# A two-layer mixer and mixture-of-experts kernel: one-hot masks issued earlier, transposes one chunk later, and the first two mixer projections walked tile by tile

## The chip, the cores and the metric

The kernel runs on one NeuronCore of a Trainium2 chip. The metric is the device time of one execution in microseconds (us): 1666.42 us, the median of three runs (1659.75 to 1669.41). Five engines work side by side, each on its own list of instructions in order: PE (TensorE, matrix products), DVE (VectorE), ACT (ScalarE), POOL (GpSimd) and SP, which here only issues transfers (DMAs). They meet through semaphores: an instruction that waits holds up all that stands behind it on its engine.

## The reference

256 tokens of width 1024 pass through two layers. Each has a token mixer and then a feed-forward part, with a residual sum and a layer norm behind both. The first layer's feed-forward part is a dense SwiGLU, the second's a mixture of 8 experts of which each token takes 2.

```python
def token_mixer(x, ...):                     # w_in is 1024 x 9992
    h = x @ w_in + b_in
    a_q, a_k, a_v, b_u, b_v, c_qk, c_v, c_o, c_i, c_f, g_pre = split(h)
    ...                                      # attention y_a, spatial gating y_b
    qk = silu(causal_depthwise_conv(c_qk, conv_w, conv_b))
    ...                                      # chunkwise mLSTM on qk: y_c
    return (gates-weighted sum of y_a @ w_br_a, y_b @ w_br_b, y_c @ w_br_c) @ w_out

def moe_swiglu(x, router_w, router_b, w1, w3, w2):
    top_v, top_i = top_k(x @ router_w + router_b, 2)
    for e in range(8):
        out = out + gates[:, e:e+1] * ((silu(x @ w1[e]) * (x @ w3[e])) @ w2[e])
```

All data are float32. One expert has three weights of 1024 x 2816.

## The kernel before, in words

**Precision and chunks.** Every weight arrives by a DMA on SP's queue as a *chunk*, mostly 128 x 2048 numbers (1 MB), in the mixers' 384-column projections 128 x 1536. `weights` (line 115) then makes two parts of it: ACT casts the raw chunk to `wh` (L123) and DVE computes the rest `wl` = raw - wh (L125). Five raw chunks can be in place (`W_RAW`), four `wh` and four `wl`. Activations are split in the same way into `xh` and `xl`, and a product is xh*wh + xl*wh + xh*wl: three matmuls for each 128 rows of the weight (`mac`, L138 to L140, in the mixers and the dense part; L967 and L969 in the experts, where half of the work, that for the *light* experts, uses two of the three terms).

**PSUM.** Two rings of four banks: `mm` for products that accumulate, `tr` for transposes and other small results. A product's first matmul waits until whoever held its bank before has been read out.

**Experts.** `route` ranks the 8 experts by their number of tokens. The four largest are *heavy* (up to 128 slots), the others *light* (up to 64), and `moe` handles four pairs of one heavy and one light. Of each pair first the up products (three column groups, heavy and light in turn, once for w1 and once for w3), then 22 down chunks, heavy and light in turn. Tokens get into an expert's slots by a product with a one-hot mask: `onehots` (L805) makes the masks `op` of a pair with four DVE instructions (L811), and `gather` (L835) multiplies them with the tokens in eight pieces (L842) that ACT copies out (L844, L845). `moe` writes the order of PE, ACT and DVE by hand: `stream` (L928) goes from *job* to job, one weight chunk each. In a step it first issues the DMA, cast and subtraction of the chunk three steps ahead, then the products of its own chunk, then the *posts* due in this step, then one piece of side work (a gather piece, for example). A post is due so many steps behind the job it hangs on:

```python
for d, f in jobs[c].post:
    due.setdefault(c + d, []).append(f)
```

At the end of an up product the posts are: the eviction at once (`heavy`, L990 to L993; `light`, L1010 to L1013); for a light w1 product its SiLU one step later (L1034); after w3 the transposes and split of the result two steps later (`heavy_out`, L1001; `light_out`, L1022). `following`, which makes the next pair's masks and adds its gather to the side work, hangs on the first heavy down chunk, due at once.

## Time and profile before

| | |
|---|---|
| median of the runs | 1666.42 us (three runs, 1659.75 to 1669.41) |
| the profiled execution | 1661.5 us, its span 1659.8 us, mean granted TensorE clock 0.974 |
| busy share of the span | PE 94%, weight loads 81%, DVE 79%, ACT 61%, POOL 1% |
| transfers | 436.77 MB, 263 GB/s on average; 371 GB/s from 940 to 1640 us |
| stages | mixer of layer 0 to about 345 us, dense feed-forward to 545, mixer of layer 1 to 905, experts to 1640, last norm and output to the end |

A row of a timeline gives the start, the duration, engine, line, operation and tiles; the bracket at its end is how long the engine stood idle before, and what ended that. [...] A DMA share of 1 means that all 16 engines of the core had a packet under way.

### The profile page before, as it was taken

To read this page: it belongs to the slowest core of one execution; us is meant where nothing else is said; L and a number is where in the kernel's file an instruction comes from. 1 tells how busy PE (TensorE), PEld (TensorE's weight loads), DVE (VectorE), ACT (ScalarE), POOL (GpSimd) and SP (SyncE) were. 2 spreads that over 40 slices of the span, in tenths; PEclk is the share of its full clock that TensorE was granted. 3 is DMA by queue.
4 is the path that set the end of the run, shared out by engine and by line. 5 is a ranking of instruction groups with operands and counts; after the bars stand their busy time and mean duration, and the time that the engine had idled before them with its cause. 6 is when DMAs were issued, how large, how long until landed. Compare 5 with 4: busy or idle time off the path is not lost. (4 is left out here: it accounts for less than half of the span.)

```text
span 1659.8 us, 20819 instructions
## 1 busy us (share of the span) xinstructions
PE 1563.7 (94%) x7796; PEld 1336.8 (81%) x7796; DVE 1307.4 (79%) x1388; ACT 1015.5 (61%) x936; POOL 21.9 (1%) x98
## 2 busy tenths in 40 slices
PE   8899999999999999999999996999979997999995
PEld 7899978888887998987887876877867776877874
DVE  6868775774455866777578798899979998899997
ACT  4454673443343343576346786878878787878773
POOL 1000000000000000000000000000000000000000
PEclk9999999999999998999999998999989998999998
DMA  8555644754554564555563999999989999999994
GB/s 290 175 172 176 224 154 139 270 176 157 201 203 133 178 200 143 185 188 162 170 217 103 358 386 361 341 387 379 356 349 401 371 375 386 346 391 377 349 415 181
DMA packets 168804, 436.77 MB, mean 263 GB/s; under 512 B 9588, under 2 KB 56824, under 8 KB 168696
## 3 DMA queue, kind: packets, MB, share of 16 engines
q1 hardware_dynamic: 168696, 435.37, 72.6%
q8 instruction: 63, 1.03, 0.2%
q14 instruction: 45, 0.37, 0.1%
HBM read 434.29 MB, written 1.05 MB: 262 GB/s over the span
## 5 line engine op out<-in xcount | busy, mean ns | idle before, releaser
L125 DVE TENSOR_TENSOR wl<-raw,wh 128x2048 fp32r<-128x2048 f32 (+3 forms) x437 | 905.9, 2095 | 216.2 <-ACT wh L123 214.7
L123 ACT CAST wh<-raw 128x2048 fp32r<-128x2048 f32 (+3 forms) x437 | 761.2, 1755 | 375.0 <-PE mm L139 264.1
L138 PE MATMUL mm<-wh,xh 128*128 128x384 f32 (+3 forms) x1056 | 386.7, 367 | 2.9 <-ACT xh L149 2.9
L139 PE MATMUL mm<-wh,xl 128*128 128x384 f32 (+3 forms) x1056 | 386.2, 366 | 1.4 <-DVE xl L150 1.4
L140 PE MATMUL mm<-wl,xh 128*128 128x384 f32 (+3 forms) x1056 | 384.1, 364 | 0.0
L967 PE MATMUL mm<-wh,xh 128*128 128x512 f32 (+2 forms) x752 | 240.4, 382 | 6.6 <-DVE g L1059 3.7
L138 PEld LDWEIGHTS mm<-wh,xh 128*128 128x128 f32 x1056 | 200.5, 190 | 23.7 <-ACT xh L149 4.0
L139 PEld LDWEIGHTS mm<-wh,xl 128*128 128x128 f32 x1056 | 200.3, 190 | 21.6 <-DVE xl L150 2.0
L140 PEld LDWEIGHTS mm<-wl,xh 128*128 128x128 f32 x1056 | 200.3, 190 | 18.8 <-issue 0.3
L969 PE MATMUL mm<-wl,xh 128*128 128x512 f32 (+2 forms) x752 | 192.9, 379 | 1.6 <-DVE wl L125 1.5
L967 PEld LDWEIGHTS mm<-wh,xh 128*128 128x128 f32 x752 | 140.7, 190 | 32.1 <-DVE g L1059 6.0
L969 PEld LDWEIGHTS mm<-wl,xh 128*128 128x128 f32 x752 | 138.7, 189 | 27.8 <-DVE wl L125 4.8
L967 PE MATMUL mm<-wh,xl 128*128 128x512 f32 (+2 forms) x368 | 138.8, 379 | 0.0
L967 PE MATMUL mm<-wh,g 128*128 128x512 f32 x352 | 89.9, 396 | 0.0
L967 PEld LDWEIGHTS mm<-wh,xl 128*128 128x128 f32 x368 | 70.3, 191 | 11.2
L967 PEld LDWEIGHTS mm<-wh,g 128*128 128x128 f32 x352 | 65.7, 190 | 13.1
L967 PE MATMUL mm<-wh,gl 128*128 128x512 f32 x176 | 51.1, 408 | 0.0
L969 PE MATMUL mm<-wl,gl 128*128 128x512 f32 x176 | 50.4, 404 | 0.0
L842 PE MATMUL tr<-op,xt 128*128 128x256 f32 x128 | 24.0, 327 | 27.0 <-DVE op L811 27.0
L969 PE MATMUL mm<-wl,g 128*128 128x512 f32 x176 | 48.3, 393 | 0.2 <-DVE wl L125 0.2
L842 PEld LDWEIGHTS tr<-op,xt 128*128 128x128 f32 x128 | 21.7, 225 | 30.4 <-DVE op L811 28.7
L139 PE MATMUL mm<-wh,m 128*128 128x512 f32 x112 | 44.3, 395 | 0.0
(268 smaller groups left out, 1484.2 us busy)
## 6 DMA issues: line engine op xcount, KB each, us to landing
raw<-in_moe_w_dram SPq DMA_DIRECT2D x220, 1024.0 KB, 7.3
raw<-in_w_in_dram SPq DMA_DIRECT2D x68, 768.0 KB, 4.3
raw<-in_moe_w_dram SPq DMA_DIRECT2D x56, 768.0 KB, 6.5
raw<-in_ffn_w_dram SPq DMA_DIRECT2D x33, 1024.0 KB, 5.0
raw<-in_w_in_dram SPq DMA_DIRECT2D x24, 1024.0 KB, 5.1
raw<-in_w_out_dram SPq DMA_DIRECT2D x8, 1024.0 KB, 5.0
bias<-in_b_in_dram SPq DMA_DIRECT2D x34, 192.0 KB, 4.9
raw<-in_w_br_c_dram SPq DMA_DIRECT2D x8, 768.0 KB, 5.2
```

What stands on the lines that cost most here:

```text
L123: nc.scalar.copy(h, raw)
L125: nc.vector.tensor_tensor(lo, raw, h.bitcast(F32), OP.subtract)
L138: nc.tensor.matmul(ps, xh, wh, start=first, stop=False)
L139: nc.tensor.matmul(ps, xl, wh, start=False, stop=False)
L140: nc.tensor.matmul(ps, xh, wl, start=False, stop=last)
L842: nc.tensor.matmul(pt[:, b].rearrange("p e s -> p (e s)"), xt[t][i][:, c:c + P], po[:, t].rearrange("p e s -> p (e s)"), start=not t, stop ...
L967: nc.tensor.matmul(ps[u], t[:, k0 + j, :], h[:, j, c], start=first and j == i == 0, stop=False)
L969: nc.tensor.matmul(ps[u], W[0][:, k0 + j, :], lo[:, j, c], start=False, stop=last and j == kk - 1)
```

## The change

There are three edits. (1) In the experts, the next pair's masks are no longer made by `following` but by a post on the eighth job from the end of the pair's up products, in the last column group; `following` itself comes one step later (due 1 in place of 0); and the transposes and the light SiLU come one step later each (3 for 2, 2 for 1). (2) In both mixers the first two projections are done by a new function `proj2`: both weights are requested first, then tile 0 is multiplied with both, then tile 1 with both, and all four evictions are written behind. (3) In layer 0 `columns` is written before `consts`.

```diff
+    def proj2(self, w, bias, c0, n, X, evicts):
+        bs, ws, ps = [], [], []
+        for i in range(2):
+            b = self.p("bias", [P, n], F32, 2)
+            with self.tc.high_priority(LEAD):
+                self.nc.sync.dma_start(b, bcast(bias[c0 + i * n:c0 + (i + 1) * n]))
+            bs.append(b)
+            ws.append(self.wchunk(w, c0 + i * n, n))
+        for t in range(NT):
+            for i in range(2):
+                o = self.mm([P, n])
+                self.gemm(o, X[t], ws[i])
+                ps.append((i, t, o))
+        for i, t, o in ps:
+            evicts[i](t, o, bs[i])
...
-    def mixer(self, l, x, X):
+    def mixer(self, l, x, X, cols=None):
...
-        cols = self.columns(l)
+        cols = cols or self.columns(l)
...
-                self.proj(w, bias, C_QK + 768 * s + 384 * i, 384, X, ev)
-                self.pump()
+                evs.append(ev)
+            if s == 0:
+                self.proj2(w, bias, C_QK, 384, X, evs)
+            else:
+                for i in range(2):
+                    self.proj(w, bias, C_QK + 768 + 384 * i, 384, X, evs[i])
+                    self.pump()
...
+    def marks(self, p):
+        return self.onehots((p, HEAVY + p), self.rslot, (self.iota, self.iota2), F32R, "o", 1)
...
-                _, xh, xl, new = self.pair(xt, p + 1)
+                xh, xl, new = self.pair(xt, p + 1, marks.pop())
...
+            if not last:
+                jobs[-8].post.append((0, lambda p=p: marks.append(self.marks(p + 1))))
...
-            dh[0].post.append((0, lambda p=p: following(p)))
+            dh[0].post.append((1, lambda p=p: following(p)))
...
-            end.append((2, light_out if e.light else heavy_out))
+            end.append((3, light_out if e.light else heavy_out))
         elif e.light:
-            end.append((1, lambda: nc.scalar.activation(e.s, e.s, AF.Silu)))
+            end.append((2, lambda: nc.scalar.activation(e.s, e.s, AF.Silu)))
...
+            cols = net.columns(0)
             net.consts()
-            X = net.mixer(0, x, X)
+            X = net.mixer(0, x, X, cols)
```

What this moves, at three places. Line numbers in the changed kernel are 22 to 27 higher in the experts and 17 higher in `mixer` (its L864 is L842 before, L994 and L996 are L967 and L969, L1038 is L1011, L1049 is L1022, L833 is L811, L556 is L539).

The first place is PE at the end of the first pair's up products: `mm_8342` and `mm_8343` are the two banks of the last light up product (`mm_8346`, `mm_8347` in the changed kernel), `g` and `gl` are what the heavy and the light down product multiply, `tr ... op, xt` is the gather. Before:

```order
L969 MATMUL mm_8343<-wl_8340,xh_7471 128x384
L967 MATMUL mm_8411<-wh_8354,g_1332_7530 128x512
...
L969 MATMUL mm_8412<-wl_8356,g_1332_7530 128x512
L842 MATMUL tr_8435<-op_8425,xt_1241_7165 128x256
...
L967 MATMUL mm_8448<-wh_8373,gl_7934 128x512
...
L969 MATMUL mm_8449<-wl_8375,gl_7934 128x512
L1022 MATMUL tr_8458<-ident_70,hs_8298 128x128 x3
L842 MATMUL tr_8464<-op_8425,xt_1242_7166 128x256
```

and in the changed kernel:

```order
L996 MATMUL mm_8347<-wl_8344,xh_7471 128x384
L994 MATMUL mm_8416<-wh_8359,g_1332_7530 128x512
...
L996 MATMUL mm_8417<-wl_8361,g_1332_7530 128x512
L994 MATMUL mm_8436<-wh_8373,gl_7952 128x512
...
L996 MATMUL mm_8437<-wl_8375,gl_7952 128x512
L864 MATMUL tr_8451<-op_8270,xt_1241_7165 128x256
...
L994 MATMUL mm_8416<-wh_8392,g_1332_7530 128x512
...
L1049 MATMUL tr_8476<-ident_70,hs_8303 128x128 x3
```

The gather's first piece now stands behind the first light down product and no longer ahead of it, and the light transposes behind the second heavy one.

The second is DVE at the same place: the four mask instructions stand behind the light eviction (L1011) and one more subtraction before:

```order
L125 TENSOR_TENSOR wl_8389<-raw_8385,wh_8387 128x2048
L1011 TENSOR_TENSOR hs_8399<-mm_8342,hs_8399 64x384
L1011 TENSOR_TENSOR hs_8399<-mm_8343,hs_8399 64x384
L1013 TENSOR_TENSOR hs_8298<-hs_8298,hs_8399 128x384
L125 TENSOR_TENSOR wl_8409<-raw_8405,wh_8407 128x2048
L811 TENSOR_SCALAR op_8425<-iota_7171,so_7292 128x128
```

and in the changed kernel fifteen rows ahead of that eviction, in the middle of the last column group:

```order
L833 TENSOR_SCALAR op_8270<-iota_7171,so_7292 128x128
...
L125 TENSOR_TENSOR wl_8279<-raw_8275,wh_8277 128x1536
...
L125 TENSOR_TENSOR wl_8394<-raw_8390,wh_8392 128x2048
L1038 TENSOR_TENSOR hs_8404<-mm_8346,hs_8404 64x384
L1038 TENSOR_TENSOR hs_8404<-mm_8347,hs_8404 64x384
L1040 TENSOR_TENSOR hs_8303<-hs_8303,hs_8404 128x384
L125 TENSOR_TENSOR wl_8414<-raw_8410,wh_8412 128x2048
```

The light eviction itself keeps its place: it stands behind the subtraction `wl_8394` as it stood behind `wl_8389`.

The third is SP's queue at the start, where `raw` are weight chunks and the three rows from `conv_w` on are the convolution's columns. Before, they stood behind the fifteenth weight chunk:

```order
L121 DMA raw_777<-in_w_in_dram 128x4x384
L121 DMA raw_839<-in_w_in_dram 128x4x392
L239 DMA m_42_255<-in_conv_w_dram 48x128
L240 DMA m_42_255<-in_conv_b_dram 12x128
L241 DMA m_42_255<-in_sg_b_dram 6x128
```

and in the changed kernel behind the sixth:

```order
L295 DMA bias_265<-in_b_in_dram 128x384
L121 DMA raw_267<-in_w_in_dram 128x4x384
L295 DMA bias_279<-in_b_in_dram 128x384
L121 DMA raw_273<-in_w_in_dram 128x4x384
...
L121 DMA raw_432<-in_w_in_dram 128x4x384
L239 DMA m_13_104<-in_conv_w_dram 48x128
L240 DMA m_13_104<-in_conv_b_dram 12x128
L241 DMA m_13_104<-in_sg_b_dram 6x128
```

PE's transpose of the columns moves with them, from behind the first tile of the fourth projection (168 matmuls) to behind 52 matmuls, and one bias row now goes out ahead of the first weight chunk.

## Rows read from the trace of the kernel before

**Rows 1.** The page: busy time of each engine, its share, and its instructions.

```profile
PE 1563.7 (94%) x7796; PEld 1336.8 (81%) x7796; DVE 1307.4 (79%) x1388; ACT 1015.5 (61%) x936; POOL 21.9 (1%) x98
```

**Rows 2.** Stages: window, length, busy PE, PEld, DVE, ACT, POOL; clock, DMA, GB/s.

```profile
560.00:628.00 68.00, 68.00 (x394) 67.31 (x394) 51.73 (x77) 35.94 (x35) 0.00 (x0) 1.00 0.64 202
940.00:1018.00 78.00, 70.44 (x338) 58.22 (x337) 76.14 (x51) 62.52 (x50) 0.00 (x0) 0.98 0.98 362
1018.00:1208.00 190.00, 174.52 (x806) 144.95 (x805) 173.66 (x116) 147.58 (x123) 0.00 (x0) 0.96 0.98 371
```

**Rows 3.** What PE waited for: total us, times, longest.

```profile
PE tr L842 <- DVE op L811: 27.0, 4, 8.2
PE tr L1022 <- DVE hs L1013: 15.2, 9, 2.1
PE tr L1001 <- DVE hs L991: 8.4, 8, 1.7
```

**Rows 4.** Timeline of PE at the second pair boundary.

```profile
1211.55 1.07 PE L969 MATMUL mm<-wl,g 128*128 128x512 f32 x4
1220.35 1.40 PE L842 MATMUL tr<-op,xt 128*128 128x256 f32 x4 [7.72 <-DVE op L811]
...
1226.44 2.01 PE L967 MATMUL mm<-wh,g 128*128 128x512 f32 x8
...
1229.20 0.64 PE L842 MATMUL tr<-op,xt 128*128 128x256 f32 x4
1229.67 1.09 PE L967 MATMUL mm<-wh,gl 128*128 128x512 f32 x4
...
1231.51 0.64 PE L842 MATMUL tr<-op,xt 128*128 128x256 f32 x4
```

**Rows 5.** Timeline of DVE and ACT at the same boundary.

```profile
1215.97 1.13 DVE L1011 TENSOR_TENSOR hs<-mm,hs 64x384 f32<-64x384 f32 x2
...
1219.82 0.87 DVE L811 TENSOR_SCALAR op<-iota,so 128x128 fp32r<-128x128 f32 x4
1224.16 2.29 DVE L125 TENSOR_TENSOR wl<-raw,wh 128x2048 fp32r<-128x2048 f32 x1 [3.47 <-ACT wh L123]
...
1221.79 0.37 ACT L844 CAST xh<-tr 128x256 fp32r<-128x256 f32 x1 [5.41 <-PE tr L842]
```

**Rows 6.** Windows as in Rows 2: stretches of low clock, and transfers.

```profile
47.28:52.22 4.94, 4.94 (x22) 4.85 (x23) 4.05 (x11) 2.90 (x6) 0.00 (x0) 0.50 0.21 62
547.46:550.60 3.14, 3.14 (x10) 3.14 (x11) 1.83 (x3) 0.44 (x1) 0.00 (x0) 0.50 0.46 123
1171.80:1175.20 3.40, 3.40 (x10) 2.62 (x10) 3.40 (x3) 3.39 (x4) 0.00 (x0) 0.50 0.80 261
1208.00:1224.00 16.00, 8.28 (x33) 6.84 (x32) 12.30 (x14) 9.94 (x11) 0.00 (x0) 0.76 1.02 421
1224.00:1234.00 10.00, 10.00 (x47) 8.43 (x47) 6.89 (x4) 7.08 (x11) 0.00 (x0) 0.88 0.55 199
1216.20:1226.40 10.20, 6.05 (x19) 5.07 (x20) 6.66 (x9) 3.00 (x5) 0.00 (x0) 0.50 0.92 379
```

**Rows 7.** Timeline of ACT, DVE, SP and PE in the first mixer's start.

```profile
19.36 1.48 ACT L123 CAST wh<-raw 128x1536 fp32r<-128x1536 f32 x1 [2.18 <-PE mm L139]
...
23.02 1.75 DVE L125 TENSOR_TENSOR wl<-raw,wh 128x1536 fp32r<-128x1536 f32 x1
...
43.27 0.50 SPq L241 DMA_DIRECT2D m<-in_sg_b_dram  x1
...
47.28 0.35 PE L243 MATMUL tr<-ident,m 66*128 66x66 f32 x1 [4.54 <-DMA m<-in_sg_b_dram]
```

**Rows 8.** Windows as in Rows 2: the first 20 us.

```profile
0.00:10.00 10.00, 3.60 (x16) 3.14 (x16) 4.43 (x12) 3.11 (x3) 4.50 (x79) 1.00 0.75 255
10.00:20.00 10.00, 8.96 (x40) 8.31 (x41) 9.48 (x9) 6.58 (x8) 0.00 (x0) 0.83 1.06 401
```

**Rows 9.** Timeline of PE in the second mixer's start.

```profile
546.16 1.06 PE L158 MATMUL tr<-ident,x 128*128 128x128 f32 x8 [2.60 <-DVE x L261]
```

## The prediction

> **What bounds the kernel now.** I read the page's busy times first, then the windows by stage, PE's waits, and last the timelines around the longest of them. PE is busy 1563.7 of 1659.8 us [rows 1], so the question is which of its idle time is on the path.

> In the mixers it is all of it: from 560 to 628 us PE is busy 68.00 of 68.00 us at full clock, 394 matmuls at 0.1726 us each, with DVE at 51.73 and transfers at 202 GB/s [rows 2]. A us of PE's idle time there is a us of the kernel.

> In the experts it isn't. From 940 to 1018 us DVE is busy 76.14 of 78.00 us (97.6%), from 1018 to 1208, one pair, 173.66 of 190.00; PE has 174.52, but its weight loads only 144.95 [rows 2]. DVE, PE and the transfers are close together, and DVE has the least slack.

> PE's longest waits are the four on the masks, 27.0 us, the longest 8.2 [rows 3]. One is the first pair's, which stays; the other three stand at the pair boundaries (1024, 1212, 1398 us), and one is in rows 4 and 5. PE ends the first heavy down chunk at 1211.55 + 1.07 = 1212.62 and starts the gather at 1220.35 [rows 4]. The masks are ready so late because they stand in DVE's queue behind two light evictions (to 1217.10) and a subtraction (L811 starts at 1219.82). Behind the gather ACT stands for 5.41 us in its copy, and so DVE waits 3.47 us for the next cast [rows 5]. [...]

> **Part 1, masks earlier, gather one step later.** The 7.72 us go, but not wholly, because something else is late next. In the new order the first light down product stands where the gather stood. It accumulates in two banks of the ring of four; the heavy down product holds the other two, and these two were the last light up product's. DVE's two readings of them (L1011) keep their place in its queue: they start at 1215.97 and end at 1217.10, the first after about 0.57 us [rows 5]. So PE waits from 1212.62 to about 1216.5: 3.9 us in place of 7.7. Before, this wait was hidden under the longer one.

> From there I lay the old durations end to end, those at full clock: a light chunk 1231.51 - 1229.67 = 1.84 us, a gather piece 1229.67 - 1229.20 = 0.47, a heavy chunk 1229.20 - 1226.44 = 2.76 [rows 4]. Light, gather, heavy, light transposes (three at some 0.1 us: 0.33) and gather, light: 1216.5 + 1.84 + 0.47 + 2.76 + 0.33 + 0.47 + 1.84 = 1224.2. The old kernel is there at 1231.51: 7.3 us saved at full clock. The clock will not be full: PE still stands for 3.9 us. The nearest rows are the 3.40 us at 0.50 around 1173, which costs 1.7, and the 4.94 us of matmuls at 0.50 behind the 4.54 us wait at 47 us, which costs 2.5 [rows 6, 7]. I take 2.1, the middle: **5.2 us for a boundary, 15.6 for three**. The bounds are 7.3 (no low clock) and 2.2 (10.20 us of low clock again, all of it under matmuls, costs 5.1).

> Can DVE and the transfers follow? If DVE went from 173.66/190 to the 97.6% it reaches before, a pair would take 177.9 us, so 12.1 could be saved; 5.2 is under that. The four mask instructions (0.87 us) are the same work 15 rows earlier [rows 5]; they wait for nothing new and push one subtraction by 0.9 us.

> Transfers run at 421 GB/s throughout the wait, and behind it fall to 199 for 10 us because the raw buffers are full [rows 6]: (1 - 199/421) x 10 = 5.3 us of transfer are lost per boundary. If the transfers alone set the pace, just these come back: 15.8 for three, about my sum. [...]

> **Part 2, transposes and SiLU one chunk later.** This takes away waits of 15.2 us (L1022, 9 times) and 8.4 us (L1001, 8 times) [rows 3]. I count nothing for it. All these waits are for DVE instructions that stand behind subtractions, in stretches where DVE is 97.6% busy [rows 2]; DVE doesn't end sooner because PE goes on meanwhile. The cover is DVE's load; if it is gone, 23.6 us and some low clock are to be had. The other bound is 0: one chunk later all readers still come later, since the last columns' results are read by the down chunks at the end of their row.

> [...] By PE's busy time alone, all of part 2 would count.

> **Part 3, first mixer.** Gone is the wait of 4.54 us for the columns, and the 4.94 us at 0.50 behind it, worth 2.5 [rows 6, 7]: 7.0. Against that: one bias of 192 KB now goes ahead of the first weights, at 401 GB/s 0.5 us [rows 8]; and a transpose of the last evicted tile stands four matmuls behind the projections, where its eviction stands behind three subtractions of 1.75 us [rows 7]; I estimate 0.5. Net **6**, bounds 2 and 7.

> Is the wait only moved? The columns now go out behind six weight chunks. Up to there 6.2 MB (two of x, 1.05; two biases, 0.4; six of 0.79) must land: 2.55 MB by 10 us, then 401 GB/s [rows 8], so at about 19 us. PE reaches the transpose after 52 matmuls, 40 of them by 20 us [rows 8]: 20 + 12 x 0.1726 = 22. Margin 3 us; the old columns landed 4.0 us after issue (43.27 to 47.28) with a weight chunk ahead [rows 7], which is what the 19 us already holds in part.

> The new function also holds all four weight buffers until PE's 59th matmul, at about 23.3 us. The fifth chunk's cast (1.48) and subtraction (1.75) then end at about 27 [rows 7], and PE needs it after 96 matmuls, at 29.7. Cover 2.7 us.

> **Part 4, second mixer.** PE stands 2.60 us for x of tile 1 and then has 3.14 us at 0.50, worth 1.6 [rows 6, 9]: 4.2. Now 17 matmuls of the second projection on tile 0 lie before it, 17 x 0.1726 = 2.9 us, more than the wait; eight more cover the split of tile 1 behind it. For what is left I take 0.2. Net **4**, bounds 2 and 4.5.

> **Sum.** 15.6 + 0 + 6 + 4 = 25.6 us. From the profiled execution, 1661.5 us (span 1659.8 and 1.7 around it), that is 1635.9; it lies 4.9 under the median of 1666.42, from which it would be 1640.8. I say 1638, between the two.

> **The rivals.**
> *DVE takes up all it can.* The light evictions come earlier too, since ACT and DVE are no longer held behind the gather, and the pair goes to 97.6% of DVE: 3 x 12.1 + 10 = 46, time 1616 to 1620. For it speaks the 3.47 us [rows 5]; against it that these evictions keep their place behind a subtraction. Chance 0.16.
> *The wait only changes its name.* PE gets to the boundary sooner, stands for the bank until DVE reads it, and the clock falls for 10.20 us again [rows 6]: 2.2 per boundary, or nothing, as the evictions come at DVE's pace: 10 to 16 in all, 1650 to 1656. For it speaks that L1011 is unmoved. Chance 0.18.
> *Slower: the columns come late in the first mixer.* Their transpose now stands in the middle of the second product on PE, and the copy behind it in DVE's queue ahead of evictions and all later subtractions; so each us by which they land after 22 us is a us of the whole kernel. Before, they landed at 47 [rows 7]; at 47 again it costs 25 and, without the 7.0 of part 3, eats up parts 1 and 4 (19.6): 1667, 5 us over the profiled execution. It decides against the change from about 42 us on. SP's place behind six chunks speaks against it. Chance 0.05.
> That the change doesn't do what it says is ruled out by the order of instructions.

> **How the numbers follow.** The forecast has 0.61, with its own range 1629 to 1648. About 0.5% (8 us) is what a measurement of this kernel can tell from no change: faster means under 1658. The forecast and the first rival lie there (0.77), and of the second about half (0.08): 0.85 faster, 0.10 same, 0.05 slower. The range takes in most of both rivals on the fast side and stops at 1657, which leaves out about 0.15.

> **What would show it.** Right: PE's wait on L811 goes down from 27.0 to about 3; in its place three waits of about 4 us before the first light down chunk, for L1011's place in DVE's queue, each followed by a shorter stretch at 0.50; L1022's and L1001's waits shrink, and DVE's share from pair to pair goes up to about 94%, no more; no wait over 1 us at the columns and at x of tile 1. Wrong: the experts 30 us shorter (DVE was not the limit), or under 6 (another wait came in), or new waits of PE for casts around 25 to 35 us.

## The result, and the profile after

The changed kernel takes 1646.69 us (median of four runs, 1640.91 to 1651.62) against 1664.99 for the kernel before: a ratio of 0.990, with a 95% interval of 0.987 to 0.993. In a second comparison it took 1641.11 (five runs) against 1664.87: 0.9855, 0.983 to 0.988. So 18 to 24 us less, where the prediction worked out 25.6 and said 1638. Its profiled execution took 1645.59 us; its span is 16.0 us shorter than that of before.

The page's busy times of the changed kernel:

```profile
PE 1566.5 (95%) x7796; PEld 1330.4 (81%) x7796; DVE 1303.5 (79%) x1388; ACT 1013.6 (62%) x936; POOL 22.3 (1%) x98
```

Beside [rows 1], PE is busy 2.8 us more, DVE 3.9 and ACT 1.9 us less: the span is shorter because PE stands idle for 77.3 us where it was 96.1. What PE waited for in the changed kernel (total us, times, longest):

```profile
PE mm L994 <- DVE hs L1038: 15.1, 4, 4.9
PE mm L996 <- DVE wl L125: 12.6, 25, 1.0
...
PE tr L864 <- DVE op L833: 2.9, 1, 2.9
...
PE tr L1049 <- DVE hs L1040: 2.6, 4, 0.7
```

Beside [rows 3]: the 27.0 us for the masks are 2.9, the first pair's. In their place the first light down product waits for its bank (L1038). The light transposes' 15.2 us are 2.6, the heavy ones' 8.4 are gone, and there are 25 short waits for weight subtractions, 12.6 us, where the kernel before had 6 of 1.7 us in all. The windows answer to [rows 2, 6]: the start of the experts, the first pair, and the low clock behind the three boundaries (columns as in rows 2; the clock is the granted share of full speed, 0.50 to 0.51 in the last three):

```profile
932.00:1009.00 77.00, 71.58 (x334) 58.84 (x333) 76.10 (x56) 62.25 (x50) 0.00 (x0) 0.96 1.00 371
1015.00:1200.00 185.00, 173.74 (x794) 141.81 (x792) 171.72 (x113) 146.18 (x122) 0.00 (x0) 0.98 0.99 374
1021.00:1024.40 3.40, 3.38 (x9) 2.71 (x10) 3.40 (x3) 1.46 (x1) 0.00 (x0) 0.51 1.03 422
1205.40:1212.20 6.80, 6.08 (x16) 4.81 (x17) 6.18 (x6) 3.36 (x5) 0.00 (x0) 0.50 1.02 408
1386.30:1393.10 6.80, 4.83 (x13) 3.85 (x14) 6.74 (x6) 3.38 (x2) 0.00 (x0) 0.50 1.03 421
```

PE at the second boundary, and DVE at the same place (start, us, what, and the idle time before with what ended it), beside [rows 4, 5]:

```profile
1200.04 1.20 PE L996 MATMUL mm<-wl,g 128*128 128x512 f32 x4 [0.20 <-DVE wl L125]
1206.12 2.24 PE L994 MATMUL mm<-wh,gl 128*128 128x512 f32 x4 [4.88 <-DVE hs L1038]
1208.16 1.91 PE L996 MATMUL mm<-wl,gl 128*128 128x512 f32 x4
1209.86 1.05 PE L864 MATMUL tr<-op,xt 128*128 128x256 f32 x4
```

```profile
1200.18 2.29 DVE L125 TENSOR_TENSOR wl<-raw,wh 128x2048 fp32r<-128x2048 f32 x1 [0.20 <-ACT wh L123]
1202.39 1.01 DVE L150 TENSOR_TENSOR g<-tr,g 128x384 fp32r<-128x384 f32 x2
1203.32 2.28 DVE L125 TENSOR_TENSOR wl<-raw,wh 128x2048 fp32r<-128x2048 f32 x1
1205.52 1.14 DVE L1038 TENSOR_TENSOR hs<-mm,hs 64x384 f32<-64x384 f32 x2
```

The wait of 7.72 us has become one of 4.88, and the gather follows without one. DVE does not idle in it: the eviction stands behind two subtractions and the split of the last heavy columns.

In the first mixer the columns go out at 14.1 us, PE transposes them at 24.21 without a wait, and two short waits are new; in the second the wait for x of tile 1 is gone, and 0.91 us for the columns has come. SP's issue, then PE's rows at these places:

```profile
14.05 0.27 SPq L241 DMA_DIRECT2D m<-in_sg_b_dram  x1
```

```profile
11.32 0.69 PE L138 MATMUL mm<-wh,xh 128*128 128x384 f32 x1 [2.96 <-ACT xh L149]
...
24.21 0.22 PE L243 MATMUL tr<-ident,m 66*128 66x66 f32 x1
...
39.45 0.52 PE L555 MATMUL tr<-ident,e 128*128 128x128 f32 x3 [0.73 <-DVE m L228]
...
46.07 0.52 PE L555 MATMUL tr<-ident,e 128*128 128x128 f32 x3 [0.82 <-DVE e L552]
...
551.78 0.25 PE L243 MATMUL tr<-ident,m 66*128 66x66 f32 x1 [0.91 <-DMA m<-in_sg_b_dram]
```

### The profile page after: what moved, and what is told of

Read it like the earlier page. It is cut to its first block, busy times and chain, and to the rows that moved or that the text cites. A ratio compares the mean times of both kernels' runs of the same rounds, so it can differ in the third digit from the quotient of the medians.

```text
span 1643.8 us, 20812 instructions
## 1 busy us (share of the span) xinstructions
PE 1566.5 (95%) x7796; PEld 1330.4 (81%) x7796; DVE 1303.5 (79%) x1388; ACT 1013.6 (62%) x936; POOL 22.3 (1%) x98
## 3 DMA queue, kind: packets, MB, share of 16 engines
HBM read 434.29 MB, written 1.05 MB: 265 GB/s over the span
## 5 line engine op out<-in xcount | busy, mean ns | idle before, releaser
L994 PE MATMUL mm<-wh,xh 128*128 128x512 f32 (+2 forms) x752 | 240.3, 382 | 9.9 <-DVE g L1086 5.9
L996 PE MATMUL mm<-wl,xh 128*128 128x512 f32 (+2 forms) x752 | 198.3, 386 | 10.6 <-DVE wl L125 9.9
L996 PEld LDWEIGHTS mm<-wl,xh 128*128 128x128 f32 x752 | 137.2, 191 | 48.9 <-DVE wl L125 27.7
L994 PEld LDWEIGHTS mm<-wh,xh 128*128 128x128 f32 x752 | 141.1, 191 | 34.7 <-DVE g L1086 8.3
L994 PE MATMUL mm<-wh,xl 128*128 128x512 f32 (+2 forms) x368 | 138.5, 378 | 0.0
L994 PE MATMUL mm<-wh,g 128*128 128x512 f32 x352 | 89.4, 395 | 0.8 <-ACT wh L123 0.8
L994 PEld LDWEIGHTS mm<-wh,xl 128*128 128x128 f32 x368 | 69.8, 190 | 11.1
L994 PEld LDWEIGHTS mm<-wh,g 128*128 128x128 f32 x352 | 65.7, 191 | 14.4 <-ACT wh L123 1.4
L994 PE MATMUL mm<-wh,gl 128*128 128x512 f32 x176 | 52.2, 413 | 14.2 <-DVE hs L1038 14.1
L996 PE MATMUL mm<-wl,gl 128*128 128x512 f32 x176 | 51.2, 409 | 2.1 <-DVE wl L125 1.9
L994 PEld LDWEIGHTS mm<-wh,gl 128*128 128x128 f32 x176 | 33.0, 196 | 22.0 <-DVE hs L1038 16.4
L996 PE MATMUL mm<-wl,g 128*128 128x512 f32 x176 | 48.4, 393 | 0.8 <-DVE wl L125 0.8
L138 PE MATMUL mm<-wh,m 128*128 128x512 f32 x112 | 44.3, 396 | 0.0
L139 PE MATMUL mm<-wh,m 128*128 128x512 f32 x112 | 44.3, 396 | 0.0
```

The costliest lines, as they stand in the source:

```text
L138: nc.tensor.matmul(ps, xh, wh, start=first, stop=False)
L139: nc.tensor.matmul(ps, xl, wh, start=False, stop=False)
L994: nc.tensor.matmul(ps[u], t[:, k0 + j, :], h[:, j, c], start=first and j == i == 0, stop=False)
L996: nc.tensor.matmul(ps[u], W[0][:, k0 + j, :], lo[:, j, c], start=False, stop=last and j == kk - 1)
```

## The experiments

Medians, and ratios to the kernel before with their 95% intervals. The kernel before had 1664.8 to 1665.1 in each of the three comparisons, so rows can be set against each other. The changed kernel itself was run for the result above (18.3 us less) and in the first of these comparisons (23.8); below, other rows are set against 1641.11, and against 1646.69 each gain over it would be 5.6 us larger.

| kernel | median us (runs) | ratio | less than before, us |
|---|---|---|---|
| changed kernel, second time | 1641.11 (5) | 0.983 to 0.988 | 23.8 |
| mixers' parts alone | 1656.71 (6) | 0.993 to 0.997 | 8.2 |
| part 1 alone | 1656.98 (7) | 0.993 to 0.997 | 7.9 |
| part 2 alone | 1658.62 (12) | 0.994 to 0.997 | 6.3 |
| changed, light eviction earlier | 1636.65 (5) | 0.981 to 0.984 | 28.4 |
| changed, three heavy down chunks first | 1621.79 (5), 1623.89 (5) | 0.972 to 0.977 | 43.3, 40.9 |
| the same, part 2 undone | 1636.23 (5) | 0.982 to 0.985 | 28.6 |
| the same, early masks undone | 1647.95 (4) | 0.989 to 0.992 | 16.9 |
| the same, one eviction earlier | 1622.73 (5) | 0.973 to 0.975 | 42.1 |
| changed, fewer subtractions | 1604.06 (4) | 0.960 to 0.965 | 61.0 |
| changed, fewer transfers | 1625.61 (4) | 0.975 to 0.978 | 39.5 |

**The changed kernel again.**

> The changed kernel once more, for its spread and for the stretch of low clock that its profile showed at 106 to 113 us, in the first mixer's transposes L370, which took back 3.0 us. Theory A (the stretch belongs to the new order): it is there again at the same place. Theory B (it comes and goes): it is gone, or stands in the second mixer, where the kernel before had one. Median by either 1641 to 1652.

The low clock at 106 us was gone and stood at 626, in the second mixer. Theory B holds: it comes and goes with the same code.

**The parts one by one.** Mixers alone (in the experts `following` and the delays as before):

> Before with the mixers' two edits alone (first two projections tile by tile, columns first); the experts as before. From the two traces the mixers should give 3.0 us at the start of the first mixer and 3.6 at the start of the second; a stretch of low clock in the mLSTM transposes of either mixer adds or takes 3 to 4.6. So 4 to 11 us under before (my forecast of these parts was 10). Rival: gains in the mixers are lost again in the experts because transfers set the pace there: under 3 us.

8.2 us less, as expected. Its one trace is 6.1 us ahead of that of before at the first up matmul of the experts, between 4 and 8 in them, and 5.9 at the end: nothing of it is lost later. Part 1 alone:

> Before with part 1 alone: masks made in the last column group, and the gather a step later; transposes and SiLU as before, mixers as before. My forecast: 15.6 us less, each boundary's wait from 7.7 to about 4 us with a low clock of 3.4 to 6.8 us behind it. Theory T (transfers set the pace of the experts; their share was 0.975 in a pair before and 0.988 in the changed kernel): what comes back is the transfers' idle time only, (0.988 - 0.975) x 186 = 2.4 us a pair, 7 to 8 in all. Theory D (DVE sets it): DVE's idle time around a boundary, 8.7 us before, goes to about 4: 12 to 15 in all.

7.9: half the forecast, as theory T had it and for another reason, below. PE's waits in it:

```profile
PE tr L1049 <- DVE hs L1040: 16.9, 9, 2.1
PE mm L994 <- DVE hs L1038: 13.8, 4, 4.0
PE tr L1028 <- DVE hs L1018: 9.1, 8, 1.7
```

The transposes' waits have grown beside [rows 3]. On PE's timeline, in the last column group ahead of the second boundary, one of them is 1.84 us:

```profile
1185.69 0.66 PE L1049 MATMUL tr<-ident,hs 128*128 128x128 f32 x4 [1.84 <-DVE hs L1040]
```

Part 2 alone:

> Before with part 2 alone: transposes and light SiLU one chunk later; masks and mixers as before. My forecast: 0, since PE's waits on L1022 and L1001 (23.6 us) turn into waits for the weight subtractions. If PE's own time sets the pace: 15 to 23 us less. Theory T: 0 to 3 us less.

6.3 (by the interval 4.3 to 9.5), over what both my forecast and theory T allow. Its waits show the exchange: the transposes' are nearly gone, the masks' are a little longer than before (27.0), and subtractions are waited for 23 times. (Here L992, L994 and L1047 are the changed kernel's L994, L996 and L1049.)

```profile
PE tr L864 <- DVE op L833: 28.7, 4, 9.1
PE mm L994 <- DVE wl L125: 11.9, 23, 1.1
...
PE tr L1047 <- DVE hs L1038: 2.8, 4, 0.9
```

The three add up to 22.4, about what the whole gives in the same comparison (23.8).

**Is the new wait on the path?** Two ways to take it away. In one the last light up product is evicted ahead of the next chunk's cast and subtraction:

```diff
+            early = 0 <= c < len(jobs) and jobs[c].early
+            if early:
+                self.step(jobs, c, due, ready)
+                due[c].pop(0)()
             if c + AHEAD < len(jobs):
```

> The changed kernel, with the light eviction of each pair's last up product (L1037, L1038, L1040) put ahead of the next weight chunk's cast and subtraction on ACT and DVE. PE's wait before the first light down product (15.1 us in four) should go from 4.9 to about 1.3 us each, and the low clock behind it be shorter. If that wait is on the path: 3 x (3.6 + 2) = 10 to 17 us less than the changed kernel. Theory T (transfers set the pace of the experts, busy 0.988 of a pair): at most the transfers' idle time around the boundaries comes back, 1 to 5 us.

In the other PE has more to do meanwhile:

```diff
-            head = 3 if last else 1
+            head = 3
```

> The changed kernel, with three heavy down chunks ahead of the first light one in every pair (one before; the last pair already had three), so that 2 x 2.76 = 5.5 us of PE's work lie over the wait for the light eviction. The wait of 4.9 us should be gone at all boundaries. Wait on the path: 12 to 20 us less than the changed kernel. Theory T: 1 to 5 us.

The first gave 4.5 us over the changed kernel, within theory T's 1 to 5, but the intervals of the two touch, so it is hardly told from nothing: the wait shrank only to 2.69 us at the second boundary, since a subtraction and the split of the heavy columns still stood ahead, and 6.8 us of low clock still followed. The second took the wait away, and gave 19.3 us, against theory T. Waits of PE, then windows (the first two pairs, and the second boundary) with three heavy chunks first:

```profile
PE mm L996 <- DVE wl L125: 13.6, 27, 0.8
PE mm L994 <- DVE hs L1038: 3.5, 1, 3.5
PE tr L1049 <- DVE hs L1040: 3.2, 7, 0.7
```

```profile
1010.00:1190.00 180.00, 175.46 (x819) 144.46 (x817) 173.33 (x116) 148.25 (x122) 0.00 (x0) 1.00 1.00 391
1190.00:1370.00 180.00, 174.34 (x811) 142.83 (x812) 174.77 (x117) 149.94 (x126) 0.00 (x0) 1.00 1.01 395
1193.00:1208.00 15.00, 14.97 (x75) 12.36 (x74) 14.90 (x12) 14.62 (x19) 0.00 (x0) 1.00 1.03 421
```

Full clock, DVE at 96 to 97% instead of 93, and transfers at 391 to 395 GB/s instead of 374, at a share that was 0.99 already. The sizes fit: PE's waits on L1038 fall by 11.6 us (15.1 to 3.5), and half of PE's 14.3 us of work at low clock (0.50 to 0.51) in the three windows above is 7.1, an estimate, together 18.7. And ACT, whose casts DVE waits for (27.8 us from 1030 to 1565 us in the changed kernel's second trace, 12.9 with three heavy chunks), is held up less by PE. From 1030 to 1565 us its casts waited 14.7 us for PE's matmuls to free split buffers in the changed kernel's second trace, and 2.6 us here; the first two lines are from that trace, the last two from three heavy chunks:

```profile
ACT wh L123 <- PE mm L994: 11.7, 16, 1.8
...
ACT wh L123 <- PE mm L996: 3.0, 3, 1.7
```

```profile
ACT wh L123 <- PE mm L996: 2.0, 3, 1.1
...
ACT wh L123 <- PE mm L994: 0.6, 1, 0.6
```

**Which of them sets the pace?** One in four weight chunks without its subtraction, and one in eight without its transfer:

```diff
+            if not sub:
+                return h, h
```

```diff
+            if load or self.old[0] != key:
                 raw = self.t("raw", [P, kk, n], F32, W_RAW)
+            else:
+                raw = self.old[1]
```

> The changed kernel, with the subtraction left out for one in four weight chunks of the experts: PE reads the rounded weights a second time there, so the remainder's product is not the right one; the matmuls are as many. DVE loses some 69 x 2.2 = 150 us of work. Theory D (DVE sets the experts' pace): 30 us less or more, down to the next limit. Theory T (transfers): under 10 us, with transfers at a share of 0.99 or over.

> The changed kernel, with one in eight weight chunks of the experts not loaded where the chunk before it has the same shape: its cast and subtraction read the buffer of the chunk before, so the weights are wrong there, and all work on the engines stays. Transfers of the experts fall by up to 12%. Theory T: 30 us less or more, down to the next limit (DVE was busy 0.93 of a pair, so some 40). Theory D: under 10 us.

Neither theory fits both. 138.6 us less of DVE's work gave 37 us over the changed kernel, as theory D had it (30 or more), but this edit also cuts PE's own waits for subtractions, from 12.6 to 3.2 us. 29.9 MB less to transfer, some 79 us at the 378 GB/s of the changed kernel's second trace (1030 to 1565 us), gave 15.5: more than theory D's 10 and half of theory T's 30. A window of each, the first without the subtractions:

```profile
1024.00:1524.00 500.00, 485.12 (x2280) 408.79 (x2279) 390.08 (x271) 418.91 (x346) 0.00 (x0) 0.99 1.01 396
```

```profile
1024.00:1534.00 510.00, 490.97 (x2273) 405.31 (x2272) 486.39 (x320) 414.58 (x346) 0.00 (x0) 0.99 0.94 341
```

With DVE at 78%, or the transfers at 341 GB/s, PE is busy for 96 to 97% of the window, so it has little idle time left to win. That this is what ends the gain is read from the windows and was not tested. Transfer, cast, subtraction and matmul are a chain over five raw and four plus four split buffers, in which PE's stalls reached the others here (14.7 us of waits of ACT's casts against 2.6, above).

**The parts again, without the boundary's wait.**

> The version with three heavy down chunks ahead of the first light one, once more, as what the next three are compared with: 1619 to 1626, no low clock at the pair boundaries.

> The same with part 2 undone: transposes and light SiLU at their old place (2 and 1 chunks behind). My prediction's view (these waits are covered by DVE's load): within 3 us of the version with three heavy chunks. Theory P (PE's waits are on the path, since a wait of 4.9 us and its low clock gave 19 us in three): PE's waits on the transposes come back, some 23 us in 17 waits, and of these some 10 to 20 are the kernel's.

Part 2 is worth 12.3 us here (1636.23 less 1623.89), so theory P holds. With the old delays PE waits for the transposes for longer than in the kernel before, 33.7 us in 22 waits (23.6 in 17 in [rows 3]):

```profile
PE tr L1049 <- DVE hs L1040: 25.4, 12, 3.3
PE tr L1028 <- DVE hs L1018: 8.3, 10, 1.4
```

> The same with the early masks undone: the next pair's masks are made by the step behind the first heavy down chunk, with the gather one chunk later than in the kernel before. PE has two heavy chunks, 5.5 us, less to wait at the gather than its 8 us: waits of 2 to 4 us at L864 if the masks' place decides, 6 to 15 us slower than with three heavy chunks. If the masks' place no longer matters: within 3 us.

24.1 us slower, three waits of up to 8.3 at the gather. I had misjudged the edit: with `following` a step later, the masks stand a chunk later in DVE's queue too, so the second heavy chunk wins nothing, and 24.1 us is what three such waits cost here.

```profile
PE tr L864 <- DVE op L833: 22.4, 3, 8.3
```

> The same, and in the first pair's last column group the first light eviction (L1038) goes ahead of one subtraction of 1.75 us; PE waits 3.5 us for it there and has 3.4 us of low clock behind. 1 to 4 us faster than with three heavy chunks, near what five rounds can tell.

1.2 us less than its neighbour, inside the intervals: not told apart.

## Why the prediction was right, and where its steps were not

**The bound.** "DVE has the least slack" was read from busy shares, and the share was no limit: DVE had been at some 92% between boundaries and went to 96 to 97% when PE stopped holding it up. Were DVE the limit of a pair, only its idle time could be won. No run with all of DVE's work speaks against that, but there were some 40 us of it (489.8 busy of 530 us from 1040 to 1570 in the trace of before). With three heavy chunks it is some 16 (489.4 of 505 from 1030 to 1535), so PE's waits had made the larger part. The rival "DVE takes up all it can", 1616 to 1620, is not this change but nearly the version with three heavy chunks: 1621.79.

**Part 1** (15.6; alone 7.9). The mechanism was as forecast: the masks' waits gone, and a wait for L1038 in their place, in part 1 alone 3.6 us at the second boundary and 4.0 at the third, where 3.9 was worked out (4.3 to 4.9 in the whole change). In part 1 alone the low clock behind it (0.50 to 0.51) lasted 3.4, 6.9 and 6.8 us, with PE busy for 3.4, 5.5 and 5.4 of that; half of it, 2.4 on average, is its cost by estimate, where I took 2.1. Over the stretch that my sum laid out, from the heavy chunk ahead to the second light one, the weight matmuls of that trace gain 6.0, 4.9 and 4.2 us, 5.0 on average for my 5.2. But that sum has a slip: by 1231.51 the old kernel has run three gather pieces, and I laid only two. The piece comes later, and where the side work is done in both kernels 5.5, 4.4 and 3.7 are left, 4.5 on average. The step that failed is the next one, "Can DVE and the transfers follow? ... 5.2 is under that": in the last column group ahead of each boundary the same trace gives back 2.2, 2.4 and 1.6 us. PE comes to the transposes and to L1038 sooner, and DVE does not. At the second boundary 1.5 of the 2.4 go in the 1.84 us wait above, just after PE had won 1.6 where the low clock at 1171.80 [rows 6] did not come; 0.9 follow where DVE makes the masks (0.87 us at 1204.40). 3 x (4.5 - 2.1) = 7.2; this trace gains 7.6 from the first pair's first up product to the last pair's. With 7.9 / 3 = 2.6 us a boundary, part 1 came nearer to the rival "The wait only changes its name" (2.2) than to my 5.2.

**Part 2** (0; alone 6.3, and 12.3 with the boundary's wait gone). This is the wrong step. I wrote that "DVE doesn't end sooner because PE goes on meanwhile". It does. With three heavy chunks, from 1030 to 1535 us, DVE is busy 488.1 us with part 2 and 481.8 without it. The path goes over ACT's queue: without part 2, ACT's copy of the light transposes (L149) waits for PE and the light SiLU (L1061) for the eviction, and the casts that DVE needs stand behind them:

```profile
ACT gl L149 <- PE tr L1049: 12.6, 7, 2.9
ACT hs L1061 <- DVE hs L1038: 8.7, 8, 2.4
```

With part 2 the first is gone and the second is 0.4; the casts' waits for split buffers that PE holds hardly differ (5.1 without, 3.3 with it). How much the transposes' place and how much the SiLU's is worth was not tried apart. The 12.3 stand in the profiled spans too (1633.6 and 1622.2), but in the one trace of part 2 alone the experts take in all as long as before within 0.5 us, so where its 6.3 lie stays open. The 23.6 us of waits did turn into 12 us of waits for subtractions, as I expected of that run, but not into nothing. Parts 1 and 2 together came to 15.6 us (1656.71 less 1641.11), just my sum, and that is luck: alone, part 1 fell short of my figure by 7.7 us and part 2 went beyond it by 6.3. Against 1646.69 the two come to 10.0.

**Part 3** (6). The 300th matmul starts at 68.4, 71.3 and 69.6 us in the three profiled executions with the old mixers, and at 64.7 to 66.6 in the eleven with the new: 4 us. The wait for the columns is gone, as are the casts' feared delays. The terms against it were too small: the first product starts at 11.3 us (10.2 before), with 2.96 us of wait ahead of it (2.16 before), and the transposes L555 wait 0.73 and 0.82 where I had estimated 0.5. That the columns come late is refuted: 14.1 us issue, 24.21 transpose, no wait.

**Part 4** (4). The stretch from the 2700th to the 3100th matmul takes 74.1 to 74.3 us with the old mixers and 70.2 to 70.9 with the new: 3.5. The 0.91 us wait for the columns was not in the working, whose upper bound of 4.5 also lies above the 4.2 that there was to win.

The mixers' parts together measured 8.2 for my 10, and 6.1 in their own trace. In the profiled execution of the change they came as -0.2 and +8.1, because a stretch of low clock had moved from the second mixer into the first: one trace would have called part 3 a failure and part 4 twice its size.

## What to carry to other kernels

A stage in which two engines and the transfers are over 90% busy, as here (PE 94%, DVE 93%, a DMA share of 0.99 in the changed kernel's first pair), may have no single bound: ask of each wait whether it holds up another engine's queue or keeps buffers from being freed, and count it if it does, whatever the busiest share is. When a wait is to go, look for what stands right behind it in the other engine's queue, and give the waiting engine work that is ready: one number in the order of chunks was worth about as much as the whole change (19 us). And take the size of a part from runs of that part, not from one pair of traces: here errors of 7.7 and 6.3 us cancelled, and the clock moved 4 us from place to place.

## What the hardware showed that I had not expected

The DMA share says little here about how much more the transfers could do: it was 0.99 at 374 GB/s, 1.00 at 391, and 1.01 at 405 in a window of the kernel with fewer subtractions:

```profile
1005.00:1190.00 185.00, 176.26 (x834) 148.57 (x833) 145.77 (x104) 155.13 (x132) 0.00 (x0) 0.98 1.01 405
```

The clock falls in the same mLSTM transposes in some executions and not in others, after the same wait of 1.2 us: in the first mixer in 6 of 14 profiled executions, in the second in 11. Here is the one in the first mixer of the changed kernel, which cost 3.0 us; behind the transposes, from 110.09 us on, the 128x384 matmuls start 0.32 us apart in it and 0.175 ahead of it:

```profile
106.27:113.10 6.83, 6.83 (x25) 5.73 (x25) 2.38 (x4) 2.00 (x2) 0.00 (x0) 0.50 0.00 0
```

Why it comes and goes was not tried and stays open.
